# A hybrid RWKV-7, S5 and product-key expert block: how the first group's gates reach the dense stage, and the last norm in halves

## The chip, the cores and the metric

One core of a Trainium2 chip runs the whole block in one launch. The metric is device time in microseconds, the median of several executions. The profile shows one execution: its span and, for each engine (PE for matmuls, PEld for weight loads, DVE for VectorE, ACT for ScalarE, POOL for GpSimd, SP for the queue that issues most DMAs), what ran when. All times below are microseconds from the start of that span.

## What is computed

For 1024 frames of width 1024 in fp32 the reference runs one residual layer: two token mixers (RWKV-7 time mixing and an S5 state-space model) behind one input projection, then an expert mixer over 16384 single-neuron experts, then a last RMSNorm. The part that matters here is the expert mixer and the norm:

```python
h = h + mixed @ w_out
# per block of 128 frames, xt = RMSNorm(h): 8 heads pick 16 of 128 x 128 experts each
e, gate = top16_of_product_keys(xt), softmax(scores)
u_sel = table_u[e]
hid = gelu(einsum('td,thkd->thk', xt, u_sel))
h = h + einsum('thk,thkd->td', gate * hid, table_v[e])
return h * rsqrt(mean(h * h) + EPS) * norm_final
```

## The kernel before

The kernel treats the eight blocks of 128 frames in two ways. Blocks 0, 6 and 7 (`GB`) gather their experts' rows from DRAM and work on DVE (`gather_steps`; 384 gathers). Blocks 1 to 5 (`DB`, 640 frames, `ND` = 5) are done densely over all 16384 experts: `dense_steps` goes over 128 chunks of 128 experts in groups of `GV` = 4. For each chunk `score` multiplies the chunk's `u` rows with the frames on PE (48 matmuls, fp32 split into a high and a low part) and takes the GELU on ACT; `weigh` multiplies by the gates `G` on DVE and splits the product into `wh` and `wl`; `values` multiplies with the chunk's `v` rows into five PSUM banks `acc`, one for each block, first for output columns 0 to 511 (n = 0) for the four chunks of a group, then for columns 512 to 1023 (n = 1). After each half DVE adds the five banks to the SBUF tile `acc` (the evictions). In the last group ACT also squares each evicted half for the final norm.

The gates of the dense blocks are made before that. `gate_table` takes a block's chosen experts `e` and gates `g`, transposes them (copies `slc`, transposes `gp`, copies `iT` and `gT`), builds one-hot matrices `oha` and `ohb` on ACT and DVE, and multiplies them on PE (`gm`) into a dense table of 128 x 128 experts for each frame. It works in chunks of 32 frames, 20 in all: a chunk is staged in `stg` (two buffers) and stored to DRAM in `gd`, 2 MB at a time. The dense stage loads `G` for four expert chunks (`gates(q)`, 1280 KB) from `gd`, into one of two tiles of a ring. For the first group (q = 0) `gates(0, b)` loads block by block, 256 KB each, as the tables are finished.

Everything is written out in the order of a planner. The kernel's parts are streams (generators run as threads); each operation goes to a list with its engine, and the planner (`Weave`) emits the operation that can start first by its own costs and due times, with a priority for each stream. What it emits is the fixed, in-order program of each engine and of the DMA queue of SP. `nc.copy` lets the planner choose ACT or DVE. The streams around the change:

- `table_stream` runs `gate_table` for blocks 1 to 5, each as soon as its retrieval (`top_stream`, on DVE) is done.
- `dense_stream` starts when the RWKV part has left its memory. It loads the frames (`dx`, ten loads), scores the first four chunks while the tables are still made, and waits for `tabled`. Then it opens the pool `dense` in the memory that tables and retrieval leave, and goes on with `weigh` for the four chunks, `gates(1)`, and the rest.
- `late_stream` (blocks 6 and 7: mixer output, norm and retrieval, tiles `y`, `h`, `w`, PSUM bank `pp`) and `gather_stream` run beside the dense stage, paced by its progress.

After the last chunk the dense stage loads the gain of the final norm (`nl`) into a tile of `G`'s ring, computes the five reciprocal roots, multiplies each block (128 x 1024) on DVE, and stores it with one DMA of 512 KB, alternating the queues of SP and ACT.

Of the kernel before, what the change touches and what calls it, by code (L numbers as in the profile page):

```python
# [24 lines left out]
AF = mybir.ActivationFunctionType  # L25
OP = mybir.AluOpType
# [5 lines left out]
D = 1024  # L32
# [4 lines left out]
DB = [1, 2, 3, 4, 5]  # L37
NG, ND = len(GB), len(DB)
TD = ND * 128
# [331 lines left out]
class Kern:  # L371
# [799 lines left out]
    def gates(self, pool):  # L1171

        nc, A = self.nc, self.A
        for o, dst in ((8, self.gbd), (0, self.gad)):
            for dt in range(8):
                x = pool.tile([128, T], F32, name=self.nm("x"), tag="pm", bufs=2)
                w = self.weight(A["wc"][14 + o + dt])
                for s in (slice(0, 512), slice(512, 1024)):
                    nc.scalar.activation(x[:, s], self.proj(self.mm(), w, self.xH, self.xL, 8, s), AF.Tanh, scale=0.5,
                                         bias=self.hcol("bg", o + dt))  # L1180
                if dst is self.gad:
                    nc.sync.dma_start(dst[dt], x)
                else:
                    for i in range(2):
                        nc.sync.dma_start(dst[i, dt], x[:, 512 * i:512 * i + 512])
# [333 lines left out]
    def gate_table(self, blk, e, g, pool):  # L1519


        nc, v = self.nc, self.nc.vector
        p = self.ps("gp", [128, 3, 128], 1, self.psg)
        for i, src in enumerate((e[:, :, 0], e[:, :, 1], g)):
            x = pool.tile([128, 128], F32, name=self.nm("slc"), tag="slc", bufs=1)
            nc.copy(x.rearrange("p (h k) -> p h k", h=8), src)
            nc.tensor.transpose(p[:, i], x, self.ident)
        iT = pool.tile([128, 2, 128], BF, name=self.nm("iT"), tag="iT", bufs=2)
        gT = pool.tile([128, 128], F32, name=self.nm("gT"), tag="gT", bufs=2)
        nc.copy(iT, p[:, 0:2])  # L1530
        nc.copy(gT, p[:, 2])
        for t32 in range(4):
            stg = pool.tile([128, 128, 32], F32, name=self.nm("stg"), tag="stg", bufs=2)
            for t16 in range(32 // TG):
                t0 = 32 * t32 + TG * t16
                shp = [128, 2, 128, TG]
                a, b = (pool.tile([128, TG, 128], F32, name=self.nm("oh" + x), tag="oh" + x, bufs=3) for x in "ab")
                turn = lambda x: x.rearrange("p m t -> p t m")
                q = pool.tile(shp, BF, name=self.nm("ohq"), tag="ohq", bufs=2)
                v.tensor_tensor(q, self.iotaM[:, None].to_broadcast(shp), iT[:, :, None, t0:t0 + TG].to_broadcast(shp), op=OP.is_equal)  # L1540
                nc.scalar.activation(a, turn(q[:, 1]), AF.Copy)
                v.tensor_tensor(b, turn(q[:, 0]), gT[:, t0:t0 + TG, None].to_broadcast([128, TG, 128]), op=OP.mult)
                for t4 in range(TG // 4):
                    ps = self.ps("gm", [128, 4, 128], GMB, self.psg)
                    for i in range(4):
                        t = 4 * t4 + i
                        nc.tensor.matmul(ps[:, i], a[:, t], b[:, t], start=True, stop=True)
                    o = TG * t16 + 4 * t4
                    nc.scalar.activation(stg[:, :, o:o + 4], ps.rearrange("p t i -> p i t"), AF.Copy)
            nc.sync.dma_start(self.gd[4 * DB.index(blk) + t32], stg)  # L1550
        self.tabled += 1


# [9 lines left out]
    def dense_steps(self, wpool, out):  # L1563

        nc, A, v = self.nc, self.A, self.nc.vector
        t = lambda n, shape, bufs, dt=F32: self.dpool.tile(list(shape), dt, name=self.nm(n), tag="de" + n, bufs=bufs)
        x = self.dx
        W, G = {}, {}
# [15 lines left out]
        def score(c, uH, uL):  # L1584
            if c % 4 == 0 and 0 < c < 124:
                gates(c // 4 + 1)
            y = W[c] = t("w", (128, TD), 1) if self.dpool else wpool.tile([128, TD], F32, name=self.nm("w"), tag="dewl", bufs=GV + 1)
            ps = [self.ps("S", [128, HT], 2, self.pss) for _ in range(NH)]
            for k in range(8):
                w = slice(128 * k, 128 * k + 128)  # L1590
                for i in range(NH):
                    s = slice(HT * i, HT * i + HT)
                    nc.tensor.matmul(ps[i], uH[:, w], x[0][:, k, s], start=(k == 0), stop=False)
                    nc.tensor.matmul(ps[i], uH[:, w], x[1][:, k, s], start=False, stop=False)
                for i in range(NH):
                    nc.tensor.matmul(ps[i], uL[:, w], x[0][:, k, HT * i:HT * i + HT], start=False, stop=(k == 7))

            for i in range(NH):
                nc.scalar.activation(y[:, HT * i:HT * i + HT], ps[i], AF.Gelu_apprx_tanh)
            if self.dpool:  # L1600
                weigh(c)

        def weigh(c):
            w, H = W[c], t("wh", (128, TD), GV + 1, F32R)
            L = wpool.tile([128, TD], F32R, name=self.nm("wl"), tag="dewl", bufs=GV + 1)
            t32 = w.rearrange("p (b t) -> p b t", t=32)
            v.tensor_tensor(t32, t32, G[c // 4][:, :, c % 4], op=OP.mult)
            nc.scalar.activation(H, w, AF.Copy)
            nc.either("tensor_tensor", L, w, H.bitcast(F32), op=OP.subtract)
            W[c] = H, L  # L1610

        def gates(q, b=None):
            if not b:
                G[q] = self.ringed("G", (128, TD // 32, 4, 32))
            bs = slice(0, TD // 32) if b is None else slice(4 * b, 4 * b + 4)
            nc.sync.dma_start(G[q][:, bs].rearrange("p b i t -> p b (i t)"),
                              self.gd[bs, :, 4 * q:4 * q + 4, :].rearrange("b p i t -> p b (i t)"))

        def values(c, n, vH, vL):
# [10 lines left out]
            if c % GV == GV - 1:  # L1630
                for b in range(ND):
                    o = acc[:, b, 512 * n:512 * n + 512]
                    v.tensor_tensor(o, ac[b], o, op=OP.add)
                    if c == 127:
                        sq = t("w", (128, TD), 1)
                        nc.scalar.activation(sq[:, :512], o, AF.Square, accum_out=st[:, n, b:b + 1])
        acps = []
        items = [(c, None) for c in range(GV)]
        for c in range(0, 128, GV):
            items += [(c + i, 0) for i in range(GV)]  # L1640
# [10 lines left out]
        for i, it in enumerate(items):  # L1651
            if i == GV:
                for c in range(GV):
                    weigh(c)
                gates(1)
            if i == GV + 1:
                acc = t("acc", (128, ND, D), 1)
                st = self.dpool.tile([128, 2, ND], F32, name="dest")
                for b in range(ND):
                    nc.sync.dma_start(acc[:, b], self.hd[128 * DB[b]:128 * DB[b] + 128, :])  # L1660
            slots = lambda k: len(self.rings.get(k, ()))
            while len(P) < min(i + 3, N) and kinds[i:len(P) + 1].count(kinds[len(P)]) <= slots(kinds[len(P)] + "h"):
                while len(R) < min(len(P) + 3, N) and kinds[len(P):len(R) + 1].count(kinds[len(R)]) <= slots(kinds[len(R)] + "r"):
                    R.append(load(items[len(R)]))
                P.append(split(*R[len(P)]))
            if it[1] is None:
                score(it[0], *P[i])
            else:
                values(*it, *P[i])
            P[i] = None  # L1670
            if i < GV - 1:
                yield 0
                continue
            if i == GV - 1:
                for b in range(ND):
                    self.weave.wait(lambda: self.tabled > b)
                    gates(0, b)
                yield 0
                continue
            at += wt[i]  # L1680
            yield at / tot
        nl = self.ringed("G", (128, TD // 32, 4, 32)).rearrange("p b i t -> p (b i t)")[:, :D]
        nc.sync.dma_start(nl, A["nl"].to_broadcast([128, D]))
        r = self.rsqrt(self.dpool, self.ssum(st[:, 0], st[:, 1]), ND, "der")
        for b in range(ND):
            y = acc[:, b]
            v.scalar_tensor_tensor(y, y, r[:, b:b + 1], nl, op0=OP.mult, op1=OP.mult)
            (nc.scalar if b % 2 else nc.sync).dma_start(out[128 * DB[b]:128 * DB[b] + 128, :], y)


    def expert_rows(self, e, pool):
# [68 lines left out]
    def build(self, ctx, out):  # L1760
        from contextlib import ExitStack
        tc, nc = self.tc, self.nc
# [18 lines left out]
        X = {}  # L1781

        fronts, pres = [], []
        self.tabled = 0
        X["need"], NDL = 2, 12
        RH, RL = [3.0, 1.5]

# [310 lines left out]
```

## Time and profile before

| | us |
|---|---|
| median of 3 runs | 3573.41 |
| lowest and highest run | 3557.26 and 3575.26 |
| the profiled execution, its own time | 3566.2 |
| its span | 3564.4 |
| busy: PE, PEld | 3257.6, 2799.5 |
| busy: DVE, ACT, POOL | 2835.2, 1285.2, 535.6 |

The span is the time from the first to the last recorded instruction; the execution's own time is 1.8 us longer. Busy times overlap between engines, and PE's is modelled, so a busy PE need not be at its peak. The dense stage takes from about 1583 to the end.

### The profile page before, as it was taken

The numbers are of one execution on the slowest core, as the hardware profiler recorded it, in microseconds if no ns is written. First come the engines' busy times: TensorE is split into PE (matmuls) and PEld (weight loads), VectorE is DVE, ScalarE is ACT, GpSimd is POOL, SyncE is SP. The second block draws the span as 40 slices with busy tenths as digits, with TensorE's granted clock in tenths as the row PEclk, the third lists the DMA queues.
The fourth block names the chain that finished last, engine by engine and source line by source line (L and its number), as shares of the span: only waits on it lengthen the run. The fifth ranks groups of instructions, "written<-read, shape, count | busy, mean of one in ns | idle before, by whom it ended". The sixth has DMA issues, their size and how long they took to land.

```text
span 3564.4 us, 59534 instructions
## 1 busy us (share of the span) xinstructions
PE 3257.6 (91%) x22415; PEld 2799.5 (79%) x22415; DVE 2835.2 (80%) x6713; ACT 1285.2 (36%) x2910; POOL 535.6 (15%) x411
## 2 busy tenths in 40 slices
PE   8999999999889787489998989989999999999997
PEld 7777787767667676478887868878898988999996
DVE  6786424547979999967899878898888888888888
ACT  4433323323332276452333223333333333333333
POOL 0000000000000000002232222222232222222221
PEclk9999999999889898799998999999999999999998
DMA  6643223465468533479987898878888888988986
GB/s 214 216 155 101 73 90 125 132 209 196 153 230 277 184 141 150 143 256 322 340 323 264 302 325 311 284 272 313 308 311 313 310 320 309 326 312 303 324 299 217
DMA packets 359952, 869.10 MB, mean 244 GB/s; under 512 B 28960, under 2 KB 175520, under 8 KB 307952
## 3 DMA queue, kind: packets, MB, share of 16 engines
q1 hardware_dynamic: 303792, 461.01, 38.6%
q0 software_dynamic: 55296, 402.68, 30.7%
q8 instruction: 176, 2.88, 0.3%
q10 hardware_dynamic: 576, 1.61, 0.1%
q14 instruction: 112, 0.92, 0.1%
HBM read 759.16 MB, written 104.86 MB: 242 GB/s over the span
## 4 chain that ended last, share of the span: by engine, by line
PE 62%; DVE 18%; DMA 11%; issue 4%; ACT 3%; SPq 1%; POOL 0%; DVEq 0%; ACTq 0%; POOLq 0%
PE S L170 19%; PE acc L170 17%; PE mm L170 11%; PE tps L170 3%; PE gl L170 2%; DVE gacc L170 2%; PE gm L170 2%; DMA vr<-in_uv_dram 2%; DMA row<-in_uv_dram,ei 2%; PE rw L170 2%; PE rs L170 2%; PE pp L170 1%; DVE row L170 1%; DVE ti L170 1%; DMA wf<-wsd 1%
## 5 line engine op out<-in xcount | busy, mean ns | idle before, releaser
L170 POOL DMA_INDIRECT row<-in_uv_dram,ei x384 | 527.8, 1374 | 1975.4 <-DVE gacc L170 1237.9
L170 PE MATMUL S<-dx,uh 128*128 128x320 f32 x4096 | 779.9, 311 | 4.2 <-ACT w L170 2.1
L170 PEld LDWEIGHTS S<-dx,uh 128*128 128x128 f32 x4096 | 649.2, 188 | 22.3 <-issue 6.8
L170 PE MATMUL acc<-vh,wh 128*128 128x512 f32 x1280 | 502.9, 402 | 57.2 <-DVE acc L170 44.4
L170 DVE SCALAR_TENSOR_TENSOR gacc<-row,hid,gacc 128x1024 f32<-128x1024 f32 x384 | 491.4, 1280 | 69.4 <-ACT hid L170 68.9
L170 PE MATMUL acc<-vl,wh 128*128 128x512 f32 x1280 | 512.1, 400 | 9.4 <-DVE vl L170 9.2
L170 PE MATMUL acc<-vh,wl 128*128 128x512 f32 x1280 | 510.4, 399 | 0.0
L170 DVE CUSTOM_DVE_ANT_0 row<-row,gx 128x1024 f32<-128x1024 f32 x384 | 467.1, 1217 | 26.5 <-DMA row<-in_uv_dram,ei 26.3
L170 PE MATMUL S<-dx,ul 128*128 128x320 f32 x2048 | 471.7, 311 | 8.1 <-DVE ul L170 8.1
L170 PEld LDWEIGHTS S<-dx,ul 128*128 128x128 f32 x2048 | 343.3, 188 | 11.3 <-DVE ul L170 9.9
L170 PEld LDWEIGHTS acc<-vh,wh 128*128 128x128 f32 x1280 | 245.2, 192 | 119.9 <-DVE acc L170 50.6
L170 PEld LDWEIGHTS acc<-vl,wh 128*128 128x128 f32 x1280 | 246.8, 193 | 58.4 <-DVE vl L170 12.4
L170 PEld LDWEIGHTS acc<-vh,wl 128*128 128x128 f32 x1280 | 246.7, 193 | 54.8 <-issue 2.0
L170 ACT ACTIVATE hid<-hid 128x1 f32<-128x1 f32 x384 | 76.8, 200 | 558.7 <-DVE hid L170 558.4
L170 ACT ACTIVATE vh<-vr 128x512 fp32r<-128x512 f32 x256 | 160.0, 627 | 312.1 <-PE acc L170 164.4
L170 DVE TENSOR_TENSOR vl<-vr,vh 128x512 fp32r<-128x512 f32 x256 | 175.4, 686 | 80.1 <-ACT vh L170 79.7
L170 DVE TENSOR_TENSOR acc<-acc,acc 128x512 f32<-128x512 f32 x320 | 212.8, 683 | 6.0 <-PE acc L170 5.4
L170 ACT ACTIVATE w<-S 128x320 f32<-128x320 f32 x256 | 100.4, 434 | 272.2 <-PE S L170 270.7
L170 PE MATMUL gm<-ohb,oha 128*128 128x128 f32 x1280 | 170.7, 285 | 25.8 <-DVE ohb L170 12.9
L170 PE MATMUL mm<-xnH,wh 128*128 128x512 f32 x480 | 193.4, 403 | 0.2 <-ACT xnH L170 0.2
L170 PE MATMUL mm<-xnH,wl 128*128 128x512 f32 x480 | 190.9, 398 | 1.3 <-DVE wl L170 1.3
L170 PE MATMUL mm<-xnL,wh 128*128 128x512 f32 x480 | 191.5, 399 | 0.0
(419 smaller groups left out, 5485.3 us busy)
## 6 DMA issues: line engine op xcount, KB each, us to landing
ur<-in_ut_dram SPq DMA_DIRECT2D x128, 512.0 KB, 6.5
vr<-in_uv_dram SPq DMA_DIRECT2D x256, 256.0 KB, 6.4
wf<-wsd SPq DMA_DIRECT2D x120, 512.0 KB, 5.3
gd<-stg SPq DMA_DIRECT2D x20, 2048.0 KB, 6.7
G<-gd SPq DMA_DIRECT2D x31, 1280.0 KB, 14.7
wsd<-sw SPq DMA_DIRECT2D x40, 512.0 KB, 3.5
wr<-in_wc_dram SPq DMA_DIRECT2D x30, 512.0 KB, 4.3
wr<-in_wg_dram SPq DMA_DIRECT2D x32, 256.0 KB, 3.3
```

Source lines behind the costliest of these rows:

```text
L170: op.alts = [(e, self.cost(e, n, outs, ins), lambda f=f, a=a, k=k: f(*a, **k)) for e, n, f, a, k in alts]
```

## The change

In the first group the gates reach `G[0]` in another way. The tile is taken from the ring when the dense generator starts; chunks of the table that are already stored by then (`self.chunks`) are loaded from `gd` one by one (64 KB each), and each later chunk is copied from `stg` into `G[0]` by ACT or DVE when it has been staged, beside its store to `gd`. The five loads of `gates(0, b)` go; the wait for `tabled` stays.

The gain `nl` is loaded at the scores of chunk 124, and the n = 0 half of the last group is multiplied by it on DVE behind each eviction and its square. At the end ACT scales the first half of each block by its reciprocal root, DVE multiplies the second half by root and gain, and each half is stored by itself: ten DMAs of 256 KB, all on SP's queue.

```diff
--- before.py
+++ after.py
@@ -1547,7 +1547,12 @@
                         nc.tensor.matmul(ps[:, i], a[:, t], b[:, t], start=True, stop=True)
                     o = TG * t16 + 4 * t4
                     nc.scalar.activation(stg[:, :, o:o + 4], ps.rearrange("p t i -> p i t"), AF.Copy)
-            nc.sync.dma_start(self.gd[4 * DB.index(blk) + t32], stg)
+            n = 4 * DB.index(blk) + t32
+            nc.sync.dma_start(self.gd[n], stg)
+            if self.g0 is None:
+                self.chunks = n + 1
+            else:
+                nc.copy(self.g0[:, n], stg[:, 0:4])
         self.tabled += 1
 
 
@@ -1584,6 +1589,9 @@
         def score(c, uH, uL):
             if c % 4 == 0 and 0 < c < 124:
                 gates(c // 4 + 1)
+            elif c == 124:
+                nl.append(self.ringed("G", (128, TD // 32, 4, 32)).rearrange("p b i t -> p (b i t)")[:, :D])
+                nc.sync.dma_start(nl[0], A["nl"].to_broadcast([128, D]))
             y = W[c] = t("w", (128, TD), 1) if self.dpool else wpool.tile([128, TD], F32, name=self.nm("w"), tag="dewl", bufs=GV + 1)
             ps = [self.ps("S", [128, HT], 2, self.pss) for _ in range(NH)]
             for k in range(8):
@@ -1609,10 +1617,10 @@
             nc.either("tensor_tensor", L, w, H.bitcast(F32), op=OP.subtract)
             W[c] = H, L
 
-        def gates(q, b=None):
-            if not b:
+        def gates(q, n=None):
+            if n is None:
                 G[q] = self.ringed("G", (128, TD // 32, 4, 32))
-            bs = slice(0, TD // 32) if b is None else slice(4 * b, 4 * b + 4)
+            bs = slice(0, TD // 32) if n is None else slice(n, n + 1)
             nc.sync.dma_start(G[q][:, bs].rearrange("p b i t -> p b (i t)"),
                               self.gd[bs, :, 4 * q:4 * q + 4, :].rearrange("b p i t -> p b (i t)"))
 
@@ -1634,7 +1642,12 @@
                     if c == 127:
                         sq = t("w", (128, TD), 1)
                         nc.scalar.activation(sq[:, :512], o, AF.Square, accum_out=st[:, n, b:b + 1])
-        acps = []
+                        if n == 0:
+                            v.tensor_tensor(o, o, nl[0][:, :512], op=OP.mult)
+        acps, nl = [], []
+        G[0] = self.g0 = self.ringed("G", (128, TD // 32, 4, 32))
+        for n in range(self.chunks):
+            gates(0, n)
         items = [(c, None) for c in range(GV)]
         for c in range(0, 128, GV):
             items += [(c + i, 0) for i in range(GV)]
@@ -1674,18 +1687,18 @@
             if i == GV - 1:
                 for b in range(ND):
                     self.weave.wait(lambda: self.tabled > b)
-                    gates(0, b)
                 yield 0
                 continue
             at += wt[i]
             yield at / tot
-        nl = self.ringed("G", (128, TD // 32, 4, 32)).rearrange("p b i t -> p (b i t)")[:, :D]
-        nc.sync.dma_start(nl, A["nl"].to_broadcast([128, D]))
         r = self.rsqrt(self.dpool, self.ssum(st[:, 0], st[:, 1]), ND, "der")
         for b in range(ND):
-            y = acc[:, b]
-            v.scalar_tensor_tensor(y, y, r[:, b:b + 1], nl, op0=OP.mult, op1=OP.mult)
-            (nc.scalar if b % 2 else nc.sync).dma_start(out[128 * DB[b]:128 * DB[b] + 128, :], y)
+            rows = slice(128 * DB[b], 128 * DB[b] + 128)
+            y0, y1 = acc[:, b, :512], acc[:, b, 512:]
+            nc.scalar.activation(y0, y0, AF.Copy, scale=r[:, b:b + 1])
+            nc.sync.dma_start(out[rows, :512], y0)
+            v.scalar_tensor_tensor(y1, y1, r[:, b:b + 1], nl[0][:, 512:], op0=OP.mult, op1=OP.mult)
+            nc.sync.dma_start(out[rows, 512:], y1)
 
 
     def expert_rows(self, e, pool):
@@ -1781,7 +1794,7 @@
         X = {}
 
         fronts, pres = [], []
-        self.tabled = 0
+        self.tabled, self.g0, self.chunks = 0, None, 0
         X["need"], NDL = 2, 12
         RH, RL = [3.0, 1.5]
```

## Rows read from the trace of the kernel before

**Rows 1.** The page's chain that ended last: share of the span by engine.

```profile
PE 62%; DVE 18%; DMA 11%; issue 4%; ACT 3%; SPq 1%; POOL 0%; DVEq 0%; ACTq 0%; POOLq 0%
```

**Rows 2.** Windows: length, busy time of each engine, granted PE clock, DMA share, GB/s.

```profile
1560.00:1640.00 80.00, 58.86 (x322) 52.49 (x321) 39.64 (x56) 20.14 (x44) 10.90 (x9) 0.87 0.93 317
1700.00:2000.00 300.00, 276.73 (x1495) 242.81 (x1494) 268.31 (x542) 97.03 (x238) 82.17 (x57) 0.94 0.85 303
2000.00:3000.00 1000.00, 951.25 (x5256) 850.92 (x5255) 856.80 (x1342) 329.17 (x793) 264.82 (x192) 0.98 0.88 308
3000.00:3500.00 500.00, 500.00 (x2813) 456.60 (x2812) 438.75 (x577) 176.98 (x422) 138.64 (x103) 1.00 0.88 311
3532.00:3550.00 18.00, 16.50 (x60) 12.14 (x60) 10.55 (x26) 7.93 (x22) 0.00 (x0) 0.86 0.42 117
3555.00:3563.00 8.00, 0.00 (x0) 0.00 (x0) 5.11 (x5) 0.00 (x0) 0.00 (x0) 0.50 0.83 328
```

**Rows 3.** The chain in order of time: start, us, engine or transfer.

```profile
1457.82 6.86 DMA ur<-in_ut_dram
...
1464.70 1.06 ACT uh L170
...
1563.92 10.72 DMA gd<-stg
...
1576.51 4.35 DMA G<-gd
...
1590.15 6.25 DMA vr<-in_uv_dram
...
3538.30 8.47 PE acc L170 x36
```

**Rows 4.** Timeline, tables to dense stage: start, us, engine, operation [idle before, releaser].

```profile
1570.19 0.77 ACT L170 ACTIVATE w<-S 128x320 f32<-128x320 f32 x2 [6.29 <-PE S L170]
...
1574.66 0.35 SPq L170 DMA_DIRECT2D h<-in_x_dram  x1
...
1577.57 4.31 SPq L170 DMA_DIRECT2D vr<-in_uv_dram  x2
...
1581.05 0.83 DVE L170 TENSOR_TENSOR w<-w,G 128x640 f32<-128x640 f32 x1 [19.98 <-DMA G<-gd]
...
1582.70 0.80 PE L170 MATMUL acc<-vh,wh 128*128 128x512 f32 x1 [12.40 <-ACT wh L170]
...
1589.45 1.40 PE L170 MATMUL acc<-vh,wh 128*128 128x512 f32 x5
```

**Rows 5.** Timeline around the start of the last two blocks' tables.

```profile
1462.18 0.47 PE L170 MATMUL gp<-ident,slc 128*128 128x128 f32 x1 [22.34 <-DVE slc L170]
...
1465.66 0.29 ACT L170 ACTIVATE slc<-e 128x128 f32<-128x128 f32 x1
...
1552.89 4.51 SPq L170 DMA_DIRECT2D G<-gd  x4
```

**Rows 6.** Tile `G`: its table loads, duration of an issue (least, median, most, ns).

```profile
L170 SPq DMA_DIRECT2D G<-gd x36: 426/478/1549, 1552.9 to 3409.1; - x36
```

**Rows 7.** Timeline of the last group's first half: evictions, squares, PE's wait.

```profile
3531.05 0.68 DVE L170 TENSOR_TENSOR acc<-acc,acc 128x512 f32<-128x512 f32 x1
...
3531.88 0.77 PE L170 MATMUL acc<-vh,wh 128*128 128x512 f32 x1 [8.93 <-DVE acc L170]
...
3537.56 0.69 DVE L170 TENSOR_TENSOR acc<-acc,acc 128x512 f32<-128x512 f32 x1
...
3538.34 0.63 ACT L170 ACTIVATE w<-acc 128x512 f32<-128x512 f32 x1 [1.16 <-DVE acc L170]
...
3538.88 0.19 ACT L170 ACTIVATION_READ_ACCUMULATOR w<-acc 128x1 f32 x1
```

**Rows 8.** Timeline of the final norm.

```profile
3554.04 6.07 DVE L170 SCALAR_TENSOR_TENSOR acc<-acc,der,G 128x1024 f32<-128x1024 f32 x5
```

**Rows 9.** DMA issues of 1576 to 1579: KB each, us to landing.

```profile
vr<-in_uv_dram SPq DMA_DIRECT2D x1, 256.0 KB, 8.4
```

## The prediction, made before the changed kernel ran

> **What bounds the kernel now.** I read the page's chain first: PE carries 62% of it, DVE 18%, DMA 11% [rows 1]. The windows then tell where. In 3000 to 3500 PE is busy all 500 us, so an earlier start of the dense stage is worth its whole length there. In 1700 to 3000 PE idles 23.3 + 48.8 = 72 us, spread over small waits. In 1560 to 1640, the passage from the tables to the dense stage, the DMA engines are 93% busy: 5.6 of 80 us are free [rows 2].
>
> The chain in order of time gives the three places that the change touches. At 1457.82 it runs through the DMA of `ur` and ScalarE's split of it (`uh`), which ends at 1465.76. At 1563.92 it goes into the last table store, 10.72 us, then the last load of `G`, 4.35 us [rows 3]. The timeline there: the last activation of the first four scores ends at 1570.96; SP holds the load of `h` until 1574.66, when that store has landed; the first multiply by `G` starts at 1581.05 after 19.98 us of idle DVE; PE resumes at 1582.70 after 12.40 us [rows 4]. The third place is the end: PE waits 8.93 us for the evictions of the first half (n = 0), and the second half starts as the banks come free [rows 7].
>
> **The gap at 1570.** Removed: five loads of `G[0]`, and the wait for the last one. The copy of the last chunk needs only `stg`, complete when its store goes out at 1563.9 [rows 3], so `G[0]` is ready at about 1564.3, and the multiplies and splits of the first chunks fit under the scores that run until 1571. Upper end of the gain: all 12.4 us. Lower end 0, if the data, not `G[0]`, set the pace. PE can do value chunk 0 at once, whose raw tile is long there; for chunk 1 it needs the next `vr`. Before, that was issued at 1577.57 behind `G` for q = 1, and landed 8.4 us later [rows 4, 9]; PE started chunk 1 at 1589.45. The late stream's `h` and weights stand ahead of it on SP, and `h` still waits for the store. If `vr` stays behind the q = 1 load it is issued half a microsecond earlier (one SP issue less), lands at 1585.5, and after 0.6 + 0.7 us of splitting PE starts at 1586.8, 2.6 us earlier. If it goes ahead of that load it is issued where the last load of `G[0]` was, at 1576.51, lands by the chain's 6.25 us for a `vr` [rows 3] at 1582.8, and PE starts at 1584.2, 5.2 us earlier. I take the middle: -4 us, ends -12.4 and 0. The DMA engines' 5.6 us of free time say the same size. Where the stall goes: `vr` is late next.
>
> **What is moved: twelve loads ahead of `ur`.** When the dense memory opens, the table stream has stored 12 of its 20 chunks, so `chunks` should be 12 and the loads twelve of 64 KB, before the first `ur` in program order. SP issues the ten `dx` loads first, and `ur` right behind them at 1457.82 [rows 3]. An issue of `G<-gd` takes 0.43 us at the least [rows 6], and four larger ones in a row took 4.51 us, 1.13 each [rows 5]. So `ur` comes 5.2 us later, at most 13.5. Queued behind it on ScalarE is the split `uh`, and behind that the second `slc` copy, with which the tables of the last two blocks start: PE had finished the transpose before it at 1462.65, the copy began at 1465.66 after `uh` [rows 5]. So 3.0 us of the present chain are this wait. If the hand-made order keeps `uh` ahead, the tables start 5.2 us later; if the planner, which now expects `ur` later, lets the copies go first, they start 3.0 us earlier, and ScalarE stalls a few us later in the stage instead. Ends -3.0 and +13.5; I take +2, between the two orders and nearer to a short stall, since the work is the same.
>
> The Trainium skill ("DMA: Bandwidth & Descriptors", section Bandwidth) speaks against such a move: batch transfers to a megabyte, one of 64 KB takes 0.95 us. That figure is for another issue path; by it as a serial cost the loads would take 11.4 us, 6.2 more than by the smallest issue here, and the sum would be that much higher if all of it reached the tables. No run here shows 64 KB loads of `G`.
>
> **What is added in the tables.** Eight copies of 128 x 128. The nearest row is `slc<-e`, 0.29 us on ACT [rows 5]: 2.3 us. The chain there alternates between PE, ACT and DVE, so some of it shows: +1, ends 0 and 2.3.
>
> **The multiply by `nl` behind the n = 0 evictions.** Five more DVE operations of 128 x 512, each in place on what ScalarE is squaring, so it waits for the square, and the next eviction stands behind it on DVE. Before, the five evictions ran from 3531.05 to 3538.25, 7.2 us, with small work of the gather between them. After, one round is: eviction 0.68, hand-over 0.1, square 0.63 with its accumulator read (0.54 later, 0.19 long: 0.73 together), hand-over 0.1, multiply about 0.6: 2.2 us; the last eviction ends 4 x 2.2 + 0.7 = 9.5 us after the first began [rows 7]. PE's last bank comes free 2.3 us later, and the second half, 36 matmuls in 8.47 us from there [rows 3], ends as much later. Ends: 0, if the gather's small work fills the waits as it did before, and +9, if PE, which waits longer, stays at 1.2 GHz: the rest of the half would take twice its 8.5 us. The granted clock over 3532 to 3550 was 0.86 [rows 2]. I take +2.3. The load of `nl`, moved to the scores of chunk 124, takes a slot of `G`'s ring as the loads of `G` do, a whole pass over the values before its use: nothing, hidden behind that pass (if it were late, its landing would count, as a `vr`'s: 6.25 us [rows 3]).
>
> **The final norm.** DVE's five products take 6.07 us, each 128 x 1024 [rows 8]. Halved between DVE and ScalarE they take some 3.4, a gain of 2.7 if nothing else bound. But the output's 2.62 MB moved in 6.6 us of full DMA (0.83 of 8 us at a mean of 328 GB/s, so 395 GB/s) [rows 2], and that begins when the first piece is ready, 0.6 us sooner. Ten issues on SP at 0.4 are 4 us, under that. So -0.5, ends -2.7 and +1.0 (the rows of 2 KB moving at the 341 GB/s of the mixed traffic in 1560 to 1640).
>
> **Sum** on the profiled execution: -4 + 2 + 1 + 2.3 - 0.5 = +0.8, from 3566.2 to 3567 us. That execution (span 3564.4) lies 7 us under the median of the runs, 3573.4, which spread from 3557 to 3575; by the median it would be 3574. I keep 3567, and call within 0.5%, 18 us, what a measurement of this kernel can't tell from no change.
>
> **Rivals.**
> The whole gap comes back: PE takes late-stream work and chunk 0 first and the data are no bound. For it: PE is full later, and DVE idled 20 us. Against it: 93% DMA. -12.4 in place of -4 gives 3558.6, less with the better order on ScalarE.
> Slower through `ur`: the loads cost 1.13 each and `uh` stays ahead of `slc`. +13.5 in place of +2 gives 3578.5. For it: `ur` is in the chain already. Against it: the loads have a quarter of the size of those that took 1.13. The other terms sum to -1.2, so the kernel gets slower as soon as the tables start more than 1.2 us later. The page's 11.4 us, named above, would give 3576.4.
> The rearrangement: the planner writes every engine's order anew, and PE's 72 us of idle time in 1700 to 3000 grow or shrink by a quarter, 18 us: 3549 or 3585. No row speaks for a sign.
> The change does not do what it says: the first products lie in memory that `stg` held, and wait for its store as `h` did, until 1574.66. PE then starts chunk 0 some 6 us earlier than before but chunk 1 only 2.6: 3568.4.
>
> **How the numbers follow.** The sum as it stands 0.40, the whole gap 0.16, slower through `ur` 0.14, rearrangement 0.10 each way, stalled products 0.10. Faster by over 0.5% are the good rearrangement, some of the whole gap and a little of the rest: 0.20. Slower: the bad one, half of the case of `ur`: 0.18. The rest, 0.62, is no change. The range reaches to both rearrangements: 3549 to 3586.
>
> **What would show it.** Right: DVE's first multiply by `G` near 1565 to 1571 on the old scale, no wait for `G<-gd` before it; PE's idle time there split, with `vr` ending it; `ur` some 5 us later behind twelve issues; n = 0 evictions 2.2 us apart; output DMA full for 6 to 7 us from the first piece. Wrong: PE running through 1570 to 1590 without waiting; PE's idle time in 1700 to 3000 moved by more than 15 us; the second half of the last group at 1.2 GHz.

## The result and the profile after

The changed kernel is slower: 3601.26 us (3594.83 to 3607.67, four runs) against 3571.18 (3557.26 to 3575.26, four runs), ratio 1.0092 [1.0067, 1.0117]. The forecast was 3567, a sum of +0.8 us that it called no change, and at most 3586. The profiled execution took 3594.83 us, its span 3593.1, 28.7 longer than before's.

Cut at work that every version has, the spans compare like this (from one profiled execution each; c4 is the start of DVE's multiply by the gates for chunk 4, counted from 0; "tables" run from the first load of `dx` to the issue of the last table store):

```
                 before  after  after-before
start to dx      1442.6 1435.1   -7.5   nothing edited before this point
tables            121.3  122.0   +0.7
last store to c0   17.1    0.3  -16.8   the gap
c0 to c4           34.7   49.7  +15.0
c4 to c64        1022.2 1034.4  +12.2
c64 to c124       837.6  855.1  +17.5
c124 to the end    88.9   96.3   +7.4
```

The gap is gone, and 15 of its 17 us are lost again in the next four chunks. Then 30 us are lost in the steady dense stage, where the change edits nothing, and 7 at the end.

How much of a row is chance? In all 18 traces of this case DVE, ACT, POOL and SP do the same work in the same order up to the first load of `dx`, and that load starts anywhere between 1434.5 and 1453.7. From c4 to c64 two runs below with before's order there (e2 and e6) take 1027.2 and 1030.3 us, so much of the 12.2 can be chance. From c64 to c124 the same two take 835.5 us each: the 17.5 are far outside that.

The timeline of after at the passage to the dense stage, for [rows 4]:

```profile
1557.15 0.32 SPq L170 DMA_DIRECT2D gd<-stg  x1
1557.16 0.31 ACT L170 ACTIVATE G<-stg 128x128 f32<-128x128 f32 x1
1557.50 0.83 DVE L170 TENSOR_TENSOR w<-w,G 128x640 f32<-128x640 f32 x1 [3.34 <-ACT G L170]
...
1563.38 0.39 PE L170 MATMUL acc<-vh,wh 128*128 128x512 f32 x1
...
1567.81 0.33 SPq L170 DMA_DIRECT2D h<-in_x_dram  x1
...
1569.65 0.94 SPq L170 DMA_DIRECT2D vr<-in_uv_dram  x2
...
1574.31 9.18 SPq L170 DMA_DIRECT2D w<-in_wo_dram  x1
...
1574.96 1.22 PE L170 MATMUL acc<-vh,wh 128*128 128x512 f32 x2 [0.75 <-ACT vh L170]
```

The copy of the last chunk ends at 1557.47 and the multiply starts at once; PE begins chunk 0 at 1563.38, not 1582.70, and chunk 1 at 1574.96, not 1589.45. Then the data are late: one issue of the late stream's `w` holds SP for 9.18 us. Ahead of it, at 1570.69 and 1573.59, SP had issued five loads of `acc` (512 KB each) and `G` for q = 1 (1280 KB): 3.9 MB, some 13 us at the 302 GB/s of 1560 to 1640, an estimate; that these bytes are what the four chunks wait for was not tested apart. PE's groups in 1555 to 1620 name the new wait:

```profile
L170 PE MATMUL pp<-y,w 128*128 128x128 f32 x40 | 8.2, 372 | 9.2 <-DMA w<-in_wo_dram 9.2
```

It was 2.7 us before. The windows of after, in the columns of [rows 2] (the last two are the places of 3532 to 3550 and 3555 to 3563 there):

```profile
1560.00:1640.00 80.00, 61.80 (x306) 53.60 (x305) 42.25 (x59) 17.46 (x40) 11.20 (x8) 0.83 0.87 302
1700.00:2000.00 300.00, 276.77 (x1514) 244.06 (x1513) 270.91 (x547) 98.03 (x242) 83.58 (x57) 0.96 0.86 306
2000.00:3000.00 1000.00, 947.07 (x5168) 843.00 (x5168) 841.89 (x1324) 327.16 (x777) 257.68 (x188) 0.97 0.86 303
3000.00:3500.00 500.00, 492.56 (x2737) 443.82 (x2735) 427.40 (x563) 173.44 (x410) 135.08 (x99) 1.00 0.86 305
3555.00:3573.00 18.00, 13.71 (x37) 9.07 (x38) 10.51 (x26) 5.58 (x15) 0.00 (x0) 0.61 0.28 87
3584.00:3592.00 8.00, 0.00 (x0) 0.00 (x0) 2.43 (x4) 2.26 (x4) 0.00 (x0) 0.50 0.88 328
```

In 3000 to 3500 PE was busy all 500 us; now 7.4 of them are idle. The stretch from c64 to c124, in before and in after:

```profile
2637.90:3475.50 837.60, 832.50 (x4672) 759.34 (x4671) 728.91 (x972) 294.66 (x700) 233.16 (x170) 1.00 0.88 312
```

```profile
2641.50:3496.60 855.10, 840.15 (x4675) 757.65 (x4676) 727.70 (x970) 295.36 (x697) 229.01 (x168) 1.00 0.86 306
```

PE's idle time went from 5.1 to 15.0 us. The other 7.6 us are busy time of the same matmuls; their ends are modelled, so their recorded starts tell more. Most scores' matmuls start 0.147 us apart, most values' matmuls 0.226. Counted beyond that, PE's starts were late by 9.7 us in before and by 26.0 in after, 17.0 of it at matmuls that waited for an eviction (none in before). PE's waits in 2600 to 3450 (us, times, longest), first in after, then in before:

```profile
PE acc L170 <- DVE acc L170: 14.4, 14, 2.1
PE acc L170 <- DVE vl L170: 1.0, 1, 1.0
```

```profile
PE S L170 <- DVE ul L170: 3.1, 2, 1.9
PE S L170 <- ACT w L170: 1.5, 2, 0.8
PE acc L170 <- DVE vl L170: 0.5, 1, 0.5
```

PE now waits for the evictions, which it never did there before. DVE's timeline in after around one such wait shows why (all five evictions of a half, with most of what the planner put between them):

```profile
2629.76 0.68 DVE L170 TENSOR_TENSOR acc<-acc,acc 128x512 f32<-128x512 f32 x1
...
2633.19 0.69 DVE L170 TENSOR_TENSOR acc<-acc,acc 128x512 f32<-128x512 f32 x1
2633.87 1.28 DVE L170 SCALAR_TENSOR_TENSOR gacc<-row,hid,gacc 128x1024 f32<-128x1024 f32 x1
2635.07 1.22 DVE L170 CUSTOM_DVE_ANT_0 row<-row,gx 128x1024 f32<-128x1024 f32 x1
...
2636.22 0.69 DVE L170 TENSOR_TENSOR acc<-acc,acc 128x512 f32<-128x512 f32 x1
2636.82 0.68 DVE L170 TENSOR_TENSOR vl<-vr,vh 128x512 fp32r<-128x512 f32 x1
2639.80 1.28 DVE L170 SCALAR_TENSOR_TENSOR gacc<-row,hid,gacc 128x1024 f32<-128x1024 f32 x1 [2.30 <-ACT hid L170]
2641.00 0.68 DVE L170 TENSOR_TENSOR acc<-acc,acc 128x512 f32<-128x512 f32 x1
2641.60 0.81 DVE L170 TENSOR_TENSOR w<-w,G 128x640 f32<-128x640 f32 x1
2642.33 0.68 DVE L170 TENSOR_TENSOR acc<-acc,acc 128x512 f32<-128x512 f32 x1
```

A product and a sum of the gather stand between two evictions; the sum waits 2.30 us for ACT's `hid`, and the eviction behind it in DVE's fixed order waits too. PE, at 2641.74, has lost 2.09 us to it.

At the end, after's timeline for [rows 7] and its chain for the last row of [rows 3]:

```profile
3554.02 0.68 DVE L170 TENSOR_TENSOR acc<-acc,acc 128x512 f32<-128x512 f32 x1
...
3554.85 0.76 PE L170 MATMUL acc<-vh,wh 128*128 128x512 f32 x1 [10.39 <-DVE acc L170]
...
3555.93 0.69 DVE L170 TENSOR_TENSOR acc<-acc,G 128x512 f32<-128x512 f32 x1 [0.27 <-ACT w L170]
...
3556.67 0.68 DVE L170 TENSOR_TENSOR acc<-acc,acc 128x512 f32<-128x512 f32 x1
...
3561.02 1.28 DVE L170 SCALAR_TENSOR_TENSOR gacc<-gacc,fstr,gx 128x1024 f32<-128x1024 f32 x1
3562.22 0.68 DVE L170 TENSOR_TENSOR acc<-acc,acc 128x512 f32<-128x512 f32 x1
...
3564.96 0.68 DVE L170 TENSOR_TENSOR acc<-acc,acc 128x512 f32<-128x512 f32 x1
```

```profile
3565.70 10.07 PE acc L170 x36
```

The five evictions take 11.6 us, not 7.2, and the 36 matmuls behind the last take 10.07, not 8.47.

### The profile page after: what moved, and what is told of

The parts are those of the page before. It is cut to its first block, busy times and chain, and to the rows that moved or that the text cites. A ratio compares the mean times of both kernels' runs of the same rounds, so it can differ in the third digit from the quotient of the medians.

```text
span 3593.1 us, 59590 instructions
## 1 busy us (share of the span) xinstructions
PE 3279.1 (91%) x22415; PEld 2811.1 (78%) x22415; DVE 2836.4 (79%) x6715; ACT 1296.6 (36%) x2926; POOL 535.7 (15%) x411
## 4 chain that ended last, share of the span: by engine, by line
PE 45%; issue 19%; DVE 18%; DMA 9%; POOL 5%; ACT 3%; SPq 1%; POOLq 0%; DVEq 0%; ACTq 0%
PE mm L170 11%; PE S L170 11%; PE acc L170 9%; POOL row L170 5%; PE tps L170 3%; DMA row<-in_uv_dram,ei 2%; PE gm L170 2%; PE gl L170 2%; DVE gacc L170 2%; PE rw L170 2%; DMA vr<-in_uv_dram 2%; PE rs L170 2%; PE pp L170 1%; DVE row L170 1%; DVE acc L170 1%
## 5 line engine op out<-in xcount | busy, mean ns | idle before, releaser
L170 DVE SCALAR_TENSOR_TENSOR gacc<-row,hid,gacc 128x1024 f32<-128x1024 f32 x384 | 491.5, 1280 | 93.0 <-ACT hid L170 92.1
L170 PEld LDWEIGHTS gm<-ohb,oha 128*128 128x128 f32 x1280 | 158.5, 198 | 46.4 <-ACT oha L170 36.1
```

The lines of the kernel that those rows point to most:

```text
L170: op.alts = [(e, self.cost(e, n, outs, ins), lambda f=f, a=a, k=k: f(*a, **k)) for e, n, f, a, k in alts]
```

## The experiments

The theory: the loss is the planner's new order of the dense stage, not the work that the change adds. The rivals: the gates' route (loads, copies, lost cover of `vr`), or the norm in halves. The kernel before ran beside each group: 3565.93, 3566.33, 3564.2 and 3564.72 us.

**The halves of the change alone.** `e1_gates_only` is the diff without its norm parts, `e2_norm_only` the norm parts alone.

> Only the gates' new route (loads, copies, no wait for G<-gd); the end of the kernel is as before. Theory of the order (the planner, told that the gates come early, writes other orders for the rest of the dense stage, and these make PE wait for evictions): about 1.006 to 1.007 of before, the change's 1.009 without the last group's 6 to 8 us. Theory of the route (loads ahead of ur, copies, early multiplies cost by themselves): the same, 1.006 to 1.007. Theory that the norm is the cause: 0.997 to 1.000.

> Only the norm's part (gain loaded at chunk 124, multiply behind the n = 0 evictions, halves at the end). By the trace of the changed kernel: evictions of the last n = 0 half spread over 11 to 12 us in place of 7.2, the end from the reciprocal roots 0.3 us shorter: about +6 us, 1.0016. If the earlier load of the gain disturbs the order well before the last group: over +10 us, with PE waits for evictions ahead of chunk 124.

Measured: 3604.62, 1.0103 [1.0075, 1.0131], and 3568.65, 0.9997 [0.998, 1.0015]. The loss comes with the gates' edit (in e1 PE waits 12.9 us for evictions in 2600 to 3450). In the traces, of the 2516 DVE instructions that before has between c4 and c124, a line-by-line comparison finds 991 in another place in e1 and none in e2. The 6 us expected of e2 are in its profiled execution (94.7 us from c124 to the end, before 88.9) but not in its median.

**The gates' route in nearly the order of before.** `e3_order_kept` has the copies and single loads, but at no planned cost, and the planner still counts the five old loads, which are not issued:

```diff
+                self.quiet("ACT", nc.scalar.real.activation, self.g0[:, n], stg[:, 0:4], AF.Copy)
...
+    def quiet(self, eng, fn, *a):
+        op = self.weave.issue((eng, "quiet", fn, a, {}))
+        op.dur, op.dma, op.alts = 0.0, False, [(eng, 0.0, op.fn)]
...
+        def planned(*a):
+            self.weave.issue(("SP", "dma_start", lambda *a: None, a, {}))
```

`e4_order_early` is the reverse: before's own five loads, planned at no cost and without their wait for the stores.

> The gates' new route alone, but with the planner told that the gates arrive when they did before (five loads that exist in the plan alone, copies and single-chunk loads at no planned cost, the loads behind the first u loads): nearly the order of before. Theory of the order: the loss is gone and what the gap gives back remains, 2 to 8 us faster than before, 0.998 to 0.9995. Theory of the route: as e1, 1.006 to 1.007.

> The kernel before with its five loads of the first gates, but with the planner told that they cost no time and don't wait for the stores: the rest of the dense stage gets an order of the new kind, while the wait on the chip stays (3 us shorter, as the last load goes ahead of the late stream's on SP). Theory of the order: away from before by 5 to 25 us, as the new order happens to fit. Theory of the route: -3 us, 0.999.

Measured: e3 3566.04, 1.0004 [0.9987, 1.0021]; e4 3607.94, 1.0118 [1.0085, 1.015]. The route without the new order costs nothing; a new order without the route costs as much as the change. (e3's DVE order differs from before's in 109 places, all ahead of c64.) In e3 the gap is gone as in after (0.3 us from the last store to c0), yet the 2 to 8 us that I expected are not gained: c0 to c4 takes 52.9 us. In e4 PE waits 10.7 us for evictions in 2600 to 3450.

**Other orders.** `n_nudged_plan` and `n_nudged_60` are the kernel before with no edit to the work: DVE's time in the planner is pushed once (at item 10, or 60); `f_plan_late` is the gates' route with the gates announced to the planner 22 us after the last copy.

```diff
+                if X["items"] == 10:
+                    wv.free["DVE"] += 1.0
```

> The kernel before with nothing changed in its work: the planner alone is told, at the tenth item of the dense stage, that VectorE is 1 us later than it thought. It writes another order (some 770 of 6055 VectorE rows moved), of the kind that the changed kernel has: a half's five evictions stand further apart, with 8.4 us of other VectorE work from first to last in place of 7.8 on average in the later half, and more gather sums right behind their own dot. Theory of the order: slower as the change is, 1.006 to 1.012, PE waits for evictions from 2600 on. Theory that the early gates or their loads cost by themselves: 0.999 to 1.001.

> The kernel of before, the planner's clock of DVE pushed by 1 us once, at item 60 in place of item 10: no work is changed. Theory (before's order is a fortunate one among orders of the same work, and most others cost about the same): slower, 1.005 to 1.012; the largest DVE work between the first and the last of a half's five evictions in the later half is 13.2 us here against 10.7. Rival (the nudge at item 10 was a single unlucky order): within 0.3% of before.

> The gates' new route alone, and the planner told that the gates come 22 us after the last copy, 12 us later than in the kernel before. Its order is of the new kind all the same. Theory of the order: 1.006 to 1.012, so the time does not depend on whether the gates are believed early or late. Theory that an early belief is what harms: 0.998 to 1.001.

Measured: 3599.28, 1.009 [1.0059, 1.0121]; 3569.72, 1.0013 [0.9995, 1.0031]; 3606.69, 1.0102 [1.007, 1.0135]. One imaginary microsecond costs 0.9%, as much as the change; the same at item 60 costs nothing that can be measured, so my expectation that nearly any other order would be worse missed, though its longest string of evictions (13.2 us of DVE work against 10.7) is longer: that figure doesn't decide. From c64 to c124 both traces lose, 25.7 us (item 10) and 11.0 (item 60), and item 60 is 7.8 shorter than before from c4 to c64, which can be chance. PE's waits in 2600 to 3450 follow, for item 10 and item 60:

```profile
PE acc L170 <- DVE acc L170: 11.3, 12, 2.7
PE S L170 <- ACT w L170: 2.1, 5, 0.7
```

```profile
PE acc L170 <- DVE vl L170: 4.1, 4, 1.3
PE S L170 <- ACT w L170: 2.9, 3, 1.3
PE acc L170 <- DVE acc L170: 2.3, 4, 0.8
```

`f_plan_late` tells one thing more: from c4 to c124 its order on DVE, ACT, POOL and SP is that of e4, which has the old route. The same order with either route costs the same, 1.0102 and 1.0118.

**Evictions preferred.** If the order of evictions is the cause, an order that puts them first must bring the changed kernel back. `g1_after_prio` and `g0_before_prio` (changed kernel and kernel before):

```diff
-                b = op.stream.bonus
+                b = op.stream.bonus if op.own is None else op.own
...
-                    v.tensor_tensor(o, ac[b], o, op=OP.add)
+                    v.tensor_tensor(o, ac[b], o, op=OP.add).own = 5.0
```

> The changed kernel, where the planner prefers the evictions of the value banks over all else that VectorE could start at the same time. Theory of the order: PE's waits for evictions in 2600 to 3450 go from 11 to under 3 us, and the loss goes with them: 0.990 to 1.000 of before. Rival: the waits go but the gather, put back, ends later and the last group waits for it: above 1.003.

> The kernel before with the same preference for evictions. Theory of the order: its own order is a fortunate one without waits from 2600 on, so it gains less than the changed kernel does, 0.992 to 1.000; then the changed kernel with the preference is 0 to 8 us faster than this one. Rival, that the change itself costs: this one is at least 0.6% faster than the changed kernel with the preference.

Measured: 3567.42, 1.0008 [0.9992, 1.0023], and 3578.04, 1.0034 [1.0014, 1.0054]. The changed kernel is back; before loses 0.3%, where I had expected a gain, and is 10.6 us behind g1, not 0 to 8. The waits for evictions are nearly gone from both, and another takes their place: the split `vl`, now behind. g1 in 1640 to 2600, then in 2600 to 3450:

```profile
PE acc L170 <- DVE vl L170: 30.0, 8, 7.1
```

```profile
PE acc L170 <- DVE vl L170: 7.2, 7, 1.1
PE S L170 <- ACT uh L170: 4.2, 4, 2.1
```

The time came back in another place than the one where it was lost: from c64 to c124 g1 takes 854.5 us and g0 858.0, as long as after (855.1); c4 to c64 shrank, to 1002.3 and 1010.4. So the lateness of evictions is what PE waited for in the slow orders, but putting evictions first doesn't by itself mend that stretch. What these runs show as the cause is the order as a whole, not that one spacing.

**Evictions and splits preferred.** `h1_prefer_two` adds the splits of `u` and `v`; `h2_prefer_all` also the multiply by the gates and the split `wl`.

```diff
-            nc.either("tensor_tensor", L, raw, H.bitcast(F32), op=OP.subtract)
+            v.tensor_tensor(L, raw, H.bitcast(F32), op=OP.subtract).own = 5.0
```

> The changed kernel with the planner preferring on DVE the evictions and the splits vl and ul of the dense stream. Theory (in g1 the evictions stopped being late and PE waited for DVE's vl instead, 30.0 us in 1640 to 2600): PE's wait for vl falls under 15 us in 1640 to 2600 and the time under g1's, 3550 to 3567, ratio 0.995 to 1.001. Rival (what is preferred pushes the next one back: the wait moves on to wl or to the multiply by the gates): as g1, 1.000 to 1.004.

> As h1, with the multiply by the gates and the split wl preferred as well, so all of the dense stream's DVE work goes before the gather's and the late stream's. Theory: PE has no wait for DVE left in 1640 to 3450, ratio 0.992 to 1.000; rival: the gather's work, pushed back, is what ends last, and the time is longer than h1's with DVE's sums of the gather after the last chunk.

Measured: h1 3520.68, 0.9882 [0.9858, 0.9906], under its own range; h2 3560.53, 0.9983 [0.9967, 0.9998]. In h2 the rival decides: from 3500 to 3560 PE does nothing and DVE works off the gather's sums; c124 to the end is 156.3 us, not 88.9.

```profile
3500.00:3560.00 60.00, 0.00 (x0) 0.00 (x0) 48.07 (x70) 12.27 (x42) 22.38 (x14) 0.50 0.80 306
```

**The change at one order.** With h1's preference DVE's order is nearly the same whether the edits are in or not (the traces of h0, h1, h3 and h4 differ in 28 of 1496 rows at most from c4 to c64, and in two at the cuts from c64 to c124), so the edits can be priced: `h0_before_two` none, `h3_gates_two` the gates' route, `h4_norm_two` the norm. `e5_kept_norm` is e3 with the norm, the whole change in before's order up to chunk 124.

> The kernel of before with the planner's preference of h1 (evictions and the splits vl and ul before other DVE work), and nothing of the change. Theory (the preference alone makes h1 fast, the change is worth nothing): ratio 0.985 to 0.992, PE without waits for DVE acc in 2600 to 3450. Rival (h1 needs the change: the earlier first products let the late stream go ahead): above 0.994.

> The preference with the gates' new route alone. Theory: the gap's 17 us between the last table store and the first multiply are gone, the four chunks after it take 15 us longer, so within 0.3% of h0. Rival (the gap is worth the -4 us or more of the prediction once PE has no other waits): 4 to 12 us under h0, 0.1 to 0.35%.

> The preference with the norm in halves alone. Theory from the tails of e2 and e5 (5.8 us more from the last chunk's multiply by the gates to the end than in the kernel before): 4 to 7 us above h0, 0.1 to 0.2%. Rival (nothing, as e2's 0.9997 said): within 2 us of h0.

> The whole change (gates loaded and copied as in the changed kernel, multiply by nl behind the n = 0 evictions, norm in halves), with the planner made to keep the order of before up to chunk 124. Theory (the loss is the planner's new order of the dense stage): no loss, ratio 1.000 within 0.004, PE waits for no eviction in 2600 to 3450; the tail from chunk 124's multiply to the end some 5 us longer than before's 88.9, given back by the stage before or lost in the noise. Rival (the two halves of the change add up to the loss when they are together): ratio near 1.009.

```
                    us       ratio to before
none      (h0)   3518.32   0.9869 [0.9843, 0.9894]
gates     (h3)   3523.05   0.9883 [0.9861, 0.9905]
norm      (h4)   3514.52   0.9855 [0.9829, 0.9881]
both      (h1)   3520.68   0.9882 [0.9858, 0.9906]
both, before's order (e5)  3577.66   1.0043 [1.0026, 1.0059]
```

The gain is the preference's; against h0 the edits move the time by -0.11% to +0.13%, inside the intervals. Neither the gates' rival (4 to 12 us gained) nor the 4 to 7 us expected of the norm shows. In h3's trace the tables take 126.5 us, in h0's 121.7; why is open. e5 is 0.4% slower, just over the 0.4% I had allowed; in its profiled execution the first load of `dx` starts 11.1 us later than before's (1453.7), ahead of all edits, and from there to the end it takes 2123.6 us, before 2121.8. No order ahead of that start differs; the mean granted clock up to it was 0.917 in e5 and 0.927 in before. But all nine runs of e5 took 3571 us or more, so chance in one execution is not the whole of it, and the cause of e5's 0.4% stays open. It is the one place where the work of the whole change, in nearly before's order, may cost something.

PE's waits in 1640 to 2600, first in before, then in h0:

```profile
PE acc L170 <- DVE acc L170: 34.5, 20, 4.3
PE acc L170 <- DVE vl L170: 8.7, 4, 4.4
```

```profile
PE acc L170 <- DVE wl L170: 17.3, 2, 11.7
PE pp L170 <- DVE mo L170: 8.2, 1, 8.2
...
PE acc L170 <- ACT vh L170: 5.0, 1, 5.0
```

The 34.5 us for evictions are gone and PE is busy 921.27 us of these 960, not 893.08; c4 to c64 takes 965.0 us instead of 1022.2. Of these 57 us, 6.7 are given back from c124 to the end (95.6 us, before 88.9).

**The multiply by `nl` taken out of the tail.** `e6_no_nl` is e2 without the five multiplies of the n = 0 half:

```diff
-                        if n == 0:
-                            v.tensor_tensor(o, o, nl[0][:, :512], op=OP.mult)
```

> The norm in halves alone, as e2, without the multiply of the n = 0 half by nl (the gain is left out of that half of the output). Theory (the five multiplies and the waits for the squares delay the evictions): the last n = 0 eviction starts 27.6 us after the last chunk's multiply by the gates, as before, not 32.2, and the end comes 54 to 55 us after it, not 60.2. Rival (the load of nl into the ring or the half stores cost it): the end stays near 60.

Measured: 3567.89, 1.0002 [0.9981, 1.0022]. Its first and last eviction of the half:

```profile
3540.83 0.69 DVE L170 TENSOR_TENSOR acc<-acc,acc 128x512 f32<-128x512 f32 x1
...
3547.80 0.68 DVE L170 TENSOR_TENSOR acc<-acc,acc 128x512 f32<-128x512 f32 x1
```

From the start of the first to the end of the last it is 7.65 us (before 7.2, e2 11.6). The last starts 28.2 us after the last chunk's multiply by the gates (before 27.6, e2 32.2), and the end follows that multiply by 56.2 us (before 54.4, e2 60.2): of the tail's 5.8 us more in e2, 4.0 are the multiplies. Of the other 1.8, some 1.0 goes with the clock: of the second half's 60 matmuls e6 has 16 over 0.5 us long, before 11, and these start 0.43 us apart instead of 0.23 (the granted clock was 0.59 in 3541 to 3546 and 0.75 in 3546 to 3551). The rest is open.

## Why the prediction was wrong

**The step that failed** is the rearrangement, priced at 18 us each way with a chance of 0.10 each, "No row speaks for a sign". It is what happened, and it measured +30 us between c4 and c124 (12.2 + 17.5): e4 and the nudge at item 10 have the loss without the edits, e3 has the gates' edit without the loss. The bound was made from the wrong stretch. A quarter of PE's 72 idle us in 1700 to 3000 says how far existing waits may move, and there they moved little, to 76 us; the loss of 17.5 us between c64 and c124 lies where PE had 5.1 us of idle time in 837.6. [rows 2] shows it full in 3000 to 3500. Idle time could only grow there, and that was the row that spoke for a sign. h0 says the same from the other side: its order takes 57 us out of c4 to c64, where PE waited, and 0.9 out of c64 to c124. Of the four new orders without a preference (the change's, e4's, the two nudges) three cost 0.9 to 1.2% and one 0.1%: the bad case was likely, not certain. Why the planner's orders come out worse than before's is not shown.

**The gap at 1570**, -4: right in direction and in place (multiply at 1557.5, which is 1564.3 counted from the last table store as in before; no wait for `G<-gd`, the data next), the size was -1.8 (-16.8 + 15.0). Counted so, PE began chunk 1 at 1581.7, 7.7 us earlier, where the prediction had 2.6 to 5.2; PE stalled for the late stream's `w`, 9.2 us in 1555 to 1620, 5.18 of them before chunk 1, and not for `vr`. The whole gap did not come back, in e3 and h3 neither: c0 to c4 takes 14.5 (e1) to 19.2 us (h3 against h0) longer wherever the gap is gone.

**Twelve loads ahead of `ur`**, +2, and **the copies**, +1: +0.7 together. `ur` went out right behind the loads; the planner let the table's copies go ahead of `uh`, the second of the two orders named. The SP queue in after:

```profile
1445.35 4.99 SPq L170 DMA_DIRECT2D dx<-xtT  x3
1450.39 7.88 SPq L170 DMA_DIRECT2D G<-gd  x12
1458.32 0.43 SPq L170 DMA_DIRECT2D ur<-in_ut_dram  x1
```

0.66 us each, between the bounds 0.43 and 1.13: the first issue took 1.67 us, the others 0.32 to 0.46. The Trainium skill ("DMA: Bandwidth & Descriptors", section Bandwidth) gives 0.95 us for one transfer of 64 KB issued from GpSimd. That is the time of the transfer and not of its issue, so the 0.66 us of issues on SP neither bear it out nor speak against it. The prediction's estimate from it as a serial cost was 11.4 us; the twelve issues took 7.88. Where the loads stood behind the first `ur` (e3), the tables took 6.4 us longer, 127.7.

**The multiply by `nl`**, +2.3: mis-sized. Evictions came 2.2 to 3.3 us apart, not 2.2, with the gather's 1.28 us sum among the work between them; e6 puts it at 4.0 us of the tail, and the medians of e2 and h4 don't show it.

**The final norm**, -0.5: from DVE's first product to the end 10.04 us, before 10.39 [rows 8], so -0.35. DMA was 0.88 busy at 328 GB/s in after's last window (before 0.83, also at 328): that fits the prediction's reading that the output sets the end.

**The rivals** "slower through `ur`" and the stalled products did not occur: the tables took 0.7 us longer, and chunk 0 began at 1563.38, while `h` waited for its store until 1567.81. Of the half at 1.2 GHz, the prediction's end of +9, a part came: 1.6 us (last section).

## What to carry to other kernels

Where a planner writes the whole program's order, an edit at one place also draws a new order for every stage behind it: before pricing the edit, run an edit that changes nothing (a microsecond in the planner's clock), and price an edit at a fixed order. Look first at the stage where the bound engine has no idle time: a new order has little to gain there and much to lose. When PE waits for its banks, put the evictions and the splits that feed it ahead of DVE's other work. Evictions alone gave nothing here, and with everything preferred the pushed-back work ended last; evictions and splits gave 1.3%, 46 us, where the whole gap was 12.4.

## What the runs showed of the hardware

One issue of a 256 KB load held SP's queue for 9.18 us in after (1574.31) where those around it take 0.3 to 0.7, with DMA 87% busy over 1560 to 1640; all later loads of that queue waited behind it, `ur` until 1583.54 and the next `vr` until 1584.54. It is no single case: before has 18 issues on SP of over 4 us, up to 14.15, and after 15, up to 12.73. All but one in each started within 7 us of a load of `G` (1280 KB) issued on the same queue. What holds them was not tested.

PE's granted clock after its wait for the last group's evictions stayed at 0.50, the 1.2 GHz level, through 3555 to 3565 while it waited for single evictions, and came to 1.00 only in 3570 to 3578; before, it had 0.51 in 3532 to 3537 and 1.00 in 3537 to 3542. In after 8 of the 36 matmuls behind the last eviction start 0.43 us apart, in before none, where the usual distance is 0.23: that is the 1.6 us between 8.47 and 10.07.
